# A gated feed forward in two phases: all up units first, then a down-projection with resident weights

## The chip, the cores and the metric

One core of one Trainium2 chip runs the whole step: one layer of a streaming encoder for 1,024 frames of a prompt and 128 frames of running streams, 1,152 columns in all. The metric is the device time of one execution in microseconds. TensorE multiplies, ScalarE and VectorE and GpSimd work element by element, SyncE issues the DMA transfers.

## The reference

Only the last part of the layer is touched by the change:

```python
h2 = rmsnorm(x, norm_ffn)                       # (T, 1024)
up = h2 @ w_up                                  # (T, 5632) = gate and value, 2816 each
c, conv_new = causal_dwconv(up, conv_left, conv_w, conv_b)   # width 3, per channel
gate, val = jnp.split(c, [D_FF], axis=-1)
x = x + (jax.nn.gelu(gate) * val) @ w_down      # w_down (2816, 1024)
y = rmsnorm(x, norm_final)
```

All is float32. The kernel splits every operand of a product into a high and a low part (types F32R) and adds three products, high by high, high by low and low by high: `mm3`, L117 to L121, three matmuls, one per line from L119 to L121. The split of a weight is a cast on ScalarE (L95) and a subtraction on GpSimd (L96), called "ap"; with "ad" the subtraction is on VectorE. An activation is split by L86 (ScalarE) and L87 (VectorE).

## The kernel before

The 2,816 hidden channels are 22 blocks of 128, m = 0 to 21. For each m, `up_unit` (L1292) loads two weight columns of 512 KB (gate and value), multiplies them with the normed input (`mh0`, `ml0`, `mh12`, `ml12`, resident in SBUF) in three chunks of 384 columns, 24 matmuls each, copies the result to E, applies the convolution on VectorE (L1313, L1314) into C, then gelu, product (L1320) and split into gh and gl, 128 hidden channels by 1,152 columns.

The down-projection takes two blocks m at a time (`down_group`, L1358). It loads their two rows of weights (512 KB each, all 1,024 outputs), and for each of the nine column tiles t and both halves of the outputs it makes a chain of six matmuls of 512 columns into one PSUM bank. VectorE adds the bank to `x1` (L1370), the residual, which stays in SBUF. The loop at the end of the kernel runs a group after every second up unit:

```python
for m in range(NU):
    up_unit(m)
    if m >= 2 and m % 2 == 0 and m < NU - 2:
        down_group([m - 2, m - 1])
    if m == NU - 1:
        down_group([NU - 4, NU - 3])
```

The group of m = 20 and 21 is the last work, and in it the final norm of each tile t follows its last addition (`final_norm` L1326, `final_half` L1335 for the last tile, whose norm is made in halves).

Raw weights pass through two buffers, the split ones through three (`load_w` L98, pool `wp`). PSUM gives `dn` four banks. All loads and stores are issued by SyncE in one order. A scheduler sets the order of the instructions on each engine; pools and buffer counts set when a tile may be overwritten.

Of the kernel before, what the change touches and what calls it, by code (L numbers as in the profile page):

```python
# [39 lines left out]
def trunk_kernel(  # L40
# [1285 lines left out]
    def final_norm(t):  # L1326
        yo = p6.tile([P, D], F32, tag="C", bufs=3, name=f"yo{t}")
        rs = rms_scale(p6, x1[t], yo, f"y{t}")

        def scale():  # L1330
            tc.keep_in_program_order(dve.scalar_tensor_tensor(yo, x1[t], rs, gfin, ALU.mult, ALU.mult))
            store_rows(yo, t, y_prompt[0], y_sample.rearrange("b t d -> t b d"))
        return scale

    def final_half(t, hf, part, pend):  # L1335
        hs = slice(hf * 512, (hf + 1) * 512)
        if hf == 0:
            part["yo"] = p6.tile([P, D], F32, tag="E", bufs=3, name=f"yo{t}")
            part["xg"] = p6.tile([P, D], F32, tag="E", bufs=3, name=f"xg{t}")
        yo, xg = part["yo"], part["xg"]  # L1340
        ssq = p6.tile([P, 1], F32, tag="ssq", bufs=4, name=f"ssq_y{t}_{hf}")
        act.activation(yo[:, hs], x1[t][:, hs], AF.Square, accum_out=ssq)
        (dve if hf else pool).tensor_tensor(xg[:, hs], x1[t][:, hs], gfin[:, hs], ALU.mult)
        if hf:
            pend()
        rs = p6.tile([P, 1], F32, tag="rs", bufs=4, name=f"rs_y{t}_{hf}")
        pool.tensor_scalar(rs, ssq, 1.0 / D, part["rs"] if hf else EPS, ALU.mult, ALU.add)
        if hf == 0:
            part["rs"] = rs
            return  # L1350
        pool.tensor_tensor(rs, rs, neg_half, ALU.pow)
        dve.tensor_scalar(yo[:, 0:512], xg[:, 0:512], rs, None, ALU.mult)
        act.activation(yo[:, hs], xg[:, hs], AF.Copy, scale=rs)
        for h_ in range(2):
            o = slice(h_ * 512, (h_ + 1) * 512)
            store_rows(yo[:, o], t, y_prompt[0, :, o], y_sample[:, :, o].rearrange("b t d -> t b d"))

    def down_group(ms, last=False):  # L1358
        ws = [load_w(lambda r: [(r, w_down[0, m * P:(m + 1) * P, :])], [D], f"wd{m}") for m in ms]
        part = {}  # L1360
        for t in range(NT):
            tk = slice(t * P, (t + 1) * P)
            for hf in range(2):
                ps = psp.tile([P, 512], F32, tag="tp" if hf else "pj", bufs=2, name=f"dn{ms[0]}_{t}_{hf}")
                hs = slice(hf * 512, (hf + 1) * 512)
                for i, m in enumerate(ms):
                    gh, gl = gts[m]
                    wh, wl = ws[i]
# [77 lines left out]
```

## Time and profile before

| | |
|---|---|
| median of 3 runs | 1756.23 us (1755.69 to 1756.74) |
| profiled execution | 1757.64 us |
| its span in the profile | 1755.9 us, so 1.7 us lie around it |
| TensorE busy | 1718.8 us, 98% |
| VectorE, ScalarE, GpSimd busy | 884.6, 744.3, 447.7 us |
| DMA | 125 MB, 71 GB/s over the span |

"Busy" counts the time in which an engine executes; matmuls overlap each other, so the distance from start to start of two matmuls tells their cost, not the length of one. In a row of the timeline, what stands in brackets is the time that the engine was idle before, and what it waited for.

### The profile page before, as it was taken

The page shows a single profiled execution, that of the slowest core. Times are in us where ns is not written, and L with a number is a line of the kernel's source. Part 1 is how long each engine was busy: PE and PEld are TensorE (multiplying, and loading weights), DVE is VectorE, ACT ScalarE, POOL GpSimd, SP SyncE. Part 2 cuts the span into 40 slices and gives each one's busy share as a digit, 9 for nine tenths or more (in the row PEclk, how much of TensorE's full clock was granted, in tenths as well). Part 3 has the DMA queues.
Part 4 walks back from the last instruction along what each step waited for, and adds up shares of the span by engine and source line. Part 5 has one row for each costly group of instructions (what it writes and reads, how often), then busy time and mean ns, then how long its engine had stood idle before and what let it go on. Part 6 is the DMA issues. An engine that isn't in the chain of part 4 may idle for free.

```text
span 1755.9 us, 24096 instructions
## 1 busy us (share of the span) xinstructions
PE 1718.8 (98%) x9721; PEld 1563.8 (89%) x9721; DVE 884.6 (50%) x1226; ACT 744.3 (42%) x1448; POOL 447.7 (25%) x508
## 2 busy tenths in 40 slices
PE   8999999999999999999999999999999999999997
PEld 7999998888798887888889898989989899898995
DVE  5350016778777775554244534445353443535356
ACT  5231117778776776543334232423323232232323
POOL 4111233211223103314313131312213131222222
PEclk9999999999999999999999999999999999999999
DMA  6112131111113127656301111111101111111112
GB/s 186 49 46 68 63 101 55 40 47 40 59 43 97 56 72 265 212 191 193 94 1 37 35 49 49 37 49 36 52 25 61 36 49 37 37 52 36 49 37 111
DMA packets 131660, 125.10 MB, mean 71 GB/s; under 512 B 7345, under 2 KB 111741, under 8 KB 131549
## 3 DMA queue, kind: packets, MB, share of 16 engines
q1 hardware_dynamic: 131549, 123.57, 22.1%
q8 instruction: 76, 1.25, 0.3%
q14 instruction: 35, 0.29, 0.1%
HBM read 101.63 MB, written 21.65 MB: 70 GB/s over the span
## 4 chain that ended last, share of the span: by engine, by line
PE 78%; DVE 12%; ACT 4%; DMA 2%; issue 2%; POOL 1%; SPq 0%; POOLq 0%; ACTq 0%; DVEq 0%
PE up L121 10%; PE up L120 10%; PE up L119 10%; PE dn L119 4%; PE dn L120 4%; PE dn L121 4%; DVE S L603 3%; PE gb L120 2%; PE gb L121 2%; PE gb L119 2%; PE avs L813 2%; PE zs L783 2%; PE ga L119 2%; PE ga L121 1%; PE o L119 1%
## 5 line engine op out<-in xcount | busy, mean ns | idle before, releaser
L119 PE MATMUL up<-mh,wup_h 128*128 128x384 f32 x1056 | 353.4, 335 | 0.0
L121 PE MATMUL up<-mh,wup_l 128*128 128x384 f32 x1056 | 353.0, 334 | 0.0
L120 PE MATMUL up<-ml,wup_h 128*128 128x384 f32 x1056 | 352.8, 334 | 0.0
L1313 DVE SCALAR_TENSOR_TENSOR C<-E,convp,C 128x128 f32<-128x128 f32 x88 | 81.0, 921 | 286.6 <-ACT C L1310 286.6
L1370 DVE TENSOR_TENSOR x<-dn,x 128x512 f32<-128x512 f32 x198 | 132.8, 687 | 149.8 <-PE dn L121 149.7
L119 PEld LDWEIGHTS up<-mh,wup_h 128*128 128x128 f32 x1056 | 198.4, 188 | 0.5
L120 PEld LDWEIGHTS up<-ml,wup_h 128*128 128x128 f32 x1056 | 198.3, 188 | 0.3
L121 PEld LDWEIGHTS up<-mh,wup_l 128*128 128x128 f32 x1056 | 198.2, 188 | 0.0
L96 POOL TENSOR_TENSOR wup_l<-wup_r,wup_h 128x1024 fp32r<-128x1024 f32 x44 | 105.1, 2398 | 283.6 <-ACT wup_h L95 244.2
L119 PE MATMUL dn<-wd_h,gh 128*128 128x512 f32 x396 | 158.3, 401 | 2.0 <-DVE x L1370 2.0
L120 PE MATMUL dn<-wd_l,gh 128*128 128x512 f32 x396 | 156.5, 395 | 1.4 <-POOL wd_l L96 1.4
L121 PE MATMUL dn<-wd_h,gl 128*128 128x512 f32 x396 | 156.3, 395 | 0.0
L95 ACT CAST wup_h<-wup_r 128x1024 fp32r<-128x1024 f32 x44 | 45.5, 1049 | 212.7 <-PE dn L121 143.2
L1309 ACT COPY E<-up 128x384 f32<-128x384 f32 (+2 forms) x176 | 65.7, 399 | 151.0 <-PE up L121 151.0
L1314 DVE SCALAR_TENSOR_TENSOR C<-E,convp,C 128x1024 f32<-128x1024 f32 x88 | 112.0, 1273 | 0.0
L119 PEld LDWEIGHTS dn<-wd_h,gh 128*128 128x128 f32 x396 | 74.2, 188 | 26.0 <-DVE x L1370 9.2
L120 PEld LDWEIGHTS dn<-wd_l,gh 128*128 128x128 f32 x396 | 74.3, 188 | 18.5 <-POOL wd_l L96 1.9
L121 PEld LDWEIGHTS dn<-wd_h,gl 128*128 128x128 f32 x396 | 74.3, 188 | 18.0
L1310 ACT ACTIVATE C<-up,convp 128x384 f32<-128x384 f32 x132 | 90.0, 681 | 0.0
L601 DVE SCALAR_TENSOR_TENSOR e<-z,e 128x384 f32<-128x384 f32 (+3 forms) x96 | 53.2, 555 | 66.2 <-ACT e L598 65.5
L119 PE MATMUL kv<-wkv_h,hTh 128*128 128x256 f32 x288 | 85.1, 296 | 0.6 <-DVE ql L502 0.5
L121 PE MATMUL kv<-wkv_h,hTl 128*128 128x256 f32 x288 | 81.4, 283 | 0.0
(296 smaller groups left out, 3889.8 us busy)
## 6 DMA issues: line engine op xcount, KB each, us to landing
wup_r<-in_w_up_dram SPq DMA_DIRECT2D x44, 512.0 KB
wd_r<-in_w_down_dram SPq DMA_DIRECT2D x22, 512.0 KB
v<-in_cache_v_dram SPq DMA_DIRECT2D x32, 256.0 KB
kr<-in_cache_k_dram SPq DMA_DIRECT2D x7, 1024.0 KB
sp_tb<-tb SPq DMA_DIRECT2D x8, 576.0 KB
out_dram<-kvst SPq DMA_DIRECT2D x72, 64.0 KB
sp_ga<-ga SPq DMA_DIRECT2D x24, 192.0 KB
tbr<-sp_tb SPq DMA_DIRECT2D x24, 192.0 KB
```

What stands on the lines that cost most here:

```text
L95: act.copy(hi, raw)
L96: (pool if how[1] == "p" else dve).tensor_tensor(lo, raw, f32(hi), ALU.subtract)
L119: pe.matmul(ps, lhsT=lh, rhs=rh, start=start, stop=False)
L120: pe.matmul(ps, lhsT=lh, rhs=rl, start=False, stop=False)
L121: pe.matmul(ps, lhsT=ll, rhs=rh, start=False, stop=stop)
L601: dve.scalar_tensor_tensor(ev, z, 0.0, ev, ALU.max, ALU.add)
L603: dve.tensor_tensor_scan(Sv[:, ::-1], ev[:, ::-1], ev[:, ::-1], init, ALU.add, ALU.bypass)
L1309: act.copy(d_, s2_)
L1310: act.activation(C[:, cs], ps, AF.Identity, scale=convp[:, 2, u:u + 1], bias=convp[:, 3, u:u + 1])
L1313: dve.scalar_tensor_tensor(C[:, 0:P], E[:, 16 - 8 * sh:EZ - 8 * sh], wv, C[:, 0:P], ALU.mult, ALU.add)
L1314: dve.scalar_tensor_tensor(C[:, P:T], E[:, EP - sh:EL - sh], wv, C[:, P:T], ALU.mult, ALU.add)
L1370: ins = dve.tensor_tensor(x1[t][:, hs], ps, x1[t][:, hs], ALU.add)
```

## The change

The feed forward becomes two phases.

- Up phase: all 22 up units in a row. Each product g (not split) is stored to `sp_g` in device memory, 22 stores of 576 KB. The residual `x1` is stored to `sp_x` when the norm ahead of the feed forward has read it (9 x 512 KB), and its room in SBUF is given up.
- Down phase: for half hf of the outputs and tile t one block, a chain of 66 matmuls (22 hidden blocks by 3) into one PSUM bank, in the order t = 0 to 8 for hf = 0, then again for hf = 1. Blocks (0,0) and (1,0) are interleaved in pieces. The weights of one half are resident in 11 pieces q of 512 KB (two hidden blocks each). For hf = 0 pieces 0 to 2 are loaded when m = 18 is done, 3 to 5 as the last up units give up the buffers of `wp`, 6 to 10 into a pool `pb` that lies where the input of the up phase was. For hf = 1 each piece is loaded again, split "ap", once block (8,0) has used the old one.
- For every block its g is loaded again from `sp_g`, in two chunks of 11 hidden blocks (128 rows of 11 runs of 512 bytes), and split (1,408 elements per partition, ScalarE and VectorE). Two sets of split tiles take turns, one in pool `pa`, one in `pb`.
- The residual comes back as `xr` (9 x 512 KB). In the second half every tile's norm is made in halves (`final_half`), the first half's sum of squares and product before the second half's addition.
- The order of TensorE's instructions in the down phase is that of the program (`manual_schedule`).

In the code of the change, `load_w` and `mm3` stand two lines lower (L100 and L119), the rest as the hunks say. What is left out at the first "..." is the old split into gh and gl, `final_norm`, the old `final_half` and `down_group`, all removed.

```diff
--- before.py
+++ after.py
@@ -72,6 +72,8 @@
 
     sp_tb = [dram.tile([P, T], F32, name=f"sp_tb{c}") for c in range(KD)]
     sp_ga = [dram.tile([P, T], F32, name=f"sp_ga{c}") for c in range(KD)]
+    sp_x = [dram.tile([P, D], F32, name=f"sp_x{t}") for t in range(NT)]
+    sp_g = dram.tile([P, NU, T], F32, name="sp_g")
     sp_at = [dram.tile([P, SEQ], F32, name=f"sp_at{c}") for c in range(4)]
 
     ident = cp.tile([P, P], F32, name="ident")
@@ -932,7 +934,8 @@
     s_h.close()
 
 
-    m12p = mk_pool("m12", "right")
+    s_m = ExitStack()
+    m12p = mk_pool("m12", "right", stack=s_m)
     C2 = T - CH
     mh12 = m12p.tile([P, KD, C2], F32R, name="mh12")
     ml12 = m12p.tile([P, KD, C2], F32R, name="ml12")
@@ -1157,10 +1160,11 @@
     s_at.close()
 
 
-    m0p = mk_pool("m0", "right")
+    m0p = mk_pool("m0", "right", stack=s_m)
     mh0 = m0p.tile([P, KD, CH], F32R, name="mh0")
     ml0 = m0p.tile([P, KD, CH], F32R, name="ml0")
-    xpool = mk_pool("x1", "right")
+    s_x = ExitStack()
+    xpool = mk_pool("x1", "right", stack=s_x)
     x1 = [xpool.tile([P, D], F32, name=f"x1_{t}") for t in range(NT)]
     s_wo = ExitStack()
     wop = mk_pool("wo", "right", stack=s_wo)
@@ -1274,6 +1278,7 @@
     conv_prep()
     for i, t in enumerate(TORD):
         out_mm(wo, 1, t)
+        sync.dma_start(sp_x[t], x1[t])
         norm2(t)
         if i >= 2:
             norm2_T(TORD[i - 2])
@@ -1281,14 +1286,17 @@
         norm2_T(t, False)
     s5.close()
     s_wo.close()
-
-
-    p6 = mk_pool("p6", "left")
+    s_x.close()
+
+
+    NP = NU // 2
+    PA, PW = 3, 3
+    pa = mk_pool("pa", "left")
+    s6 = ExitStack()
+    p6 = mk_pool("p6", "left", stack=s6)
     EZ = 16 + P
     EP = EZ + 2
     EL = EP + SEQ
-    gts = {}
-
     def up_unit(m):
         cc = []
         for s_ in range(2):
@@ -1317,63 +1325,32 @@
             pool.tensor_copy(convq[:, u, :], E[:, EL - 2:EL])
             cc.append(C)
         act.activation(cc[0], cc[0], AF.Gelu_apprx_tanh)
-        dve.tensor_tensor(cc[0], cc[0], cc[1], ALU.mult)
-        gh = p6.tile([P, T], F32R, tag="gh", bufs=3, name=f"gh{m}")
-        gl = p6.tile([P, T], F32R, tag="gl", bufs=3, name=f"gl{m}")
-        split(gh, gl, cc[0])
-        gts[m] = (gh, gl)
-
...
+        g = p6.tile([P, T], F32, tag="g", bufs=2, name=f"g{m}")
+        dve.tensor_tensor(g, cc[0], cc[1], ALU.mult)
+        sync.dma_start(sp_g[:, m, :], g)
+
+    wds = {}
+    pools = {}
+
+    def wd_load(q, hf):
+        alt = (pa, "dh", "dl", PA) if q < PA else (wp, "hi", "lo", 3) if q < PA + PW else \
+            (pools["b"], "dh", "dl", NP - PA - PW)
+        src = w_down[0, 2 * q * P:(2 * q + 2) * P, hf * 512:(hf + 1) * 512].rearrange("(j p) d -> p j d", p=P)
+        wds[q, hf] = load_w(lambda r: [(r, src)], [2, 512], f"wd{q}_{hf}", "ap" if q < PA or hf else "ad", alt)
+
+    gts = {}
+    GC = 11
+
+    def g_load(t, hf, m0, m1):
+        nm = f"g{t}_{hf}"
+        if (t, hf) not in gts:
+            gp = pools["b"] if (t + hf) % 2 else pa
+            gts[t, hf] = [gp.tile([P, NU, P], F32R, tag=f"gg{i}", bufs=1, name=f"{nm}_{i}") for i in range(2)]
+        gh, gl = gts[t, hf]
+        raw = pa.tile([P, GC, P], F32, tag="graw", bufs=2, name=f"{nm}_r{m0}")[:, :m1 - m0, :]
+        sync.dma_start(raw, sp_g[:, m0:m1, t * P:(t + 1) * P])
+        act.copy(gh[:, m0:m1, :], raw)
+        dve.tensor_tensor(gl[:, m0:m1, :], raw, f32(gh[:, m0:m1, :]), ALU.subtract)
 
     def conv_out(rows, n, stores, nm):
         ps = psp.tile([P, P], F32, tag="av", bufs=1, name=f"tr_{nm}")
@@ -1398,19 +1375,93 @@
 
     for m in range(NU):
         up_unit(m)
-        if m >= 2 and m % 2 == 0 and m < NU - 2:
-            down_group([m - 2, m - 1])
-        if m == NU - 1:
-            down_group([NU - 4, NU - 3])
         if m in (8, 16):
             conv_rows(0, m - 8)
             conv_rows(1, m - 8)
+        if m == 18:
+            for q in range(PA):
+                wd_load(q, 0)
+            g_load(0, 0, 0, GC)
+    s_m.close()
+
+
+    pb = mk_pool("pb", "right")
+    pools["b"] = pb
+    g_load(0, 0, GC, NU - 2)
+    g_load(1, 0, 0, GC)
+    for q in range(PA, NP - 1):
+        wd_load(q, 0)
+    g_load(1, 0, GC, NU - 2)
+    wd_load(NP - 1, 0)
+    g_load(0, 0, NU - 2, NU)
+    g_load(1, 0, NU - 2, NU)
     conv_rows(0, 16)
     conv_rows(1, 16)
     conv_last()
-    gfin = p6.tile([P, D], F32, tag="E", bufs=3, name="gfin")
+    s6.close()
+    p8 = mk_pool("p8", "left")
+    gfin = p8.tile([P, D], F32, name="gfin")
     sync.dma_start(gfin, norm_final.rearrange("(o d) -> o d", o=1).to_broadcast([P, D]))
-    down_group([NU - 2, NU - 1], last=True)
+    xr = [p8.tile([P, D], F32, name=f"xr{t}") for t in range(NT)]
+    for t in range(NT):
+        sync.dma_start(xr[t], sp_x[t])
+    dps = {}
+
+    def down_mm(t, hf, qs):
+        if qs[0] == 0:
+            dps[t, hf] = psp.tile([P, 512], F32, tag="tp" if t % 2 else "pj", bufs=2, name=f"dn{t}_{hf}")
+        gh, gl = gts[t, hf]
+        for q in qs:
+            wh, wl = wds[q, hf]
+            for j in range(2):
+                m = 2 * q + j
+                mm3(dps[t, hf], gh[:, m, :], gl[:, m, :], wh[:, j, :], wl[:, j, :], m == 0, m == NU - 1)
+
+    def down_add(t, hf):
+        hs = slice(hf * 512, (hf + 1) * 512)
+        dve.tensor_tensor(xr[t][:, hs], dps.pop((t, hf)), xr[t][:, hs], ALU.add)
+
+    fin = {}
+
+    def final_half(t, hf):
+        hs = slice(hf * 512, (hf + 1) * 512)
+        if hf == 0:
+            fin[t] = [p8.tile([P, D], F32, tag=tg, bufs=2, name=f"{tg}{t}") for tg in ("yo", "xg")]
+        yo, xg = fin[t][:2]
+        ssq = p8.tile([P, 1], F32, tag="ssq", bufs=4, name=f"ssq_y{t}_{hf}")
+        act.activation(yo[:, hs], xr[t][:, hs], AF.Square, accum_out=ssq)
+        (dve if hf else pool).tensor_tensor(xg[:, hs], xr[t][:, hs], gfin[:, hs], ALU.mult)
+        rs = p8.tile([P, 1], F32, tag="rs", bufs=4, name=f"rs_y{t}_{hf}")
+        pool.tensor_scalar(rs, ssq, 1.0 / D, fin[t][2] if hf else EPS, ALU.mult, ALU.add)
+        if hf == 0:
+            fin[t].append(rs)
+            return
+        pool.tensor_tensor(rs, rs, neg_half, ALU.pow)
+        dve.tensor_scalar(yo[:, 0:512], xg[:, 0:512], rs, None, ALU.mult)
+        act.activation(yo[:, hs], xg[:, hs], AF.Copy, scale=rs)
+        for h_ in range(2):
+            o = slice(h_ * 512, (h_ + 1) * 512)
+            store_rows(yo[:, o], t, y_prompt[0, :, o], y_sample[:, :, o].rearrange("b t d -> t b d"))
+
+    with tc.manual_schedule(engines={mybir.EngineType.PE}):
+        for qs in ((0, 1, 2), (3, 4), (5, 6), (7, 8), (9,), (10,)):
+            for t in (0, 1):
+                down_mm(t, 0, qs)
+        down_add(0, 0)
+        down_add(1, 0)
+        for hf in range(2):
+            for t in range(2 * (1 - hf), NT):
+                g_load(t, hf, 0, GC)
+                g_load(t, hf, GC, NU)
+                for q in range(NP):
+                    down_mm(t, hf, (q,))
+                    if hf == 0 and t == NT - 1:
+                        wd_load(q, 1)
+                if hf:
+                    final_half(t, 0)
+                down_add(t, hf)
+                if hf:
+                    final_half(t, 1)
 
 
 _INS = ['x_prompt', 'x_sample', 'cache_k', 'cache_v', 'state_pool', 'state_conv',
```

Three places of the order are spoken of below. The first is VectorE after the last up matmul. Before, it has the additions of `dn` around the last conv chain (E and C are the tiles of one up column):

```order
L1370 TENSOR_TENSOR x_0_8139<-dn_0_0_15011,x_0_8139 128x512
L1313 SCALAR_TENSOR_TENSOR C_14902<-E_14901,convp,C_14902 128x128
L1314 SCALAR_TENSOR_TENSOR C_14902<-E_14901,convp,C_14902 128x1024
L1313 SCALAR_TENSOR_TENSOR C_14902<-E_14901,convp,C_14902 128x128
L1314 SCALAR_TENSOR_TENSOR C_14902<-E_14901,convp,C_14902 128x1024
L1370 TENSOR_TENSOR x_0_8139<-dn_0_1_15019,x_0_8139 128x512
L1320 TENSOR_TENSOR C_14804<-C_14804,C_14902 128x1152
L1370 TENSOR_TENSOR x_1_8140<-dn_1_0_15027,x_1_8140 128x512
L1370 TENSOR_TENSOR x_1_8140<-dn_1_1_15035,x_1_8140 128x512
```

Now the same place has weight splits of pieces q (`wd_0`, half 0), the last conv chain, and the low parts of g for the first two blocks (`g_0_1`: half 0, low part):

```order
L98 TENSOR_TENSOR wd_0_l<-wd_0_r,wd_0_h 128x1024
L1321 SCALAR_TENSOR_TENSOR C_13503<-E_13502,convp,C_13503 128x128
L1322 SCALAR_TENSOR_TENSOR C_13503<-E_13502,convp,C_13503 128x1024
L1321 SCALAR_TENSOR_TENSOR C_13503<-E_13502,convp,C_13503 128x128
L1322 SCALAR_TENSOR_TENSOR C_13503<-E_13502,convp,C_13503 128x1024
L1353 TENSOR_TENSOR g_0_1_13608<-g_0_r_13609,g_0_0_13607 128x1408
L1329 TENSOR_TENSOR g_13595<-C_13405,C_13503 128x1152
L98 TENSOR_TENSOR wd_0_l<-wd_0_r,wd_0_h 128x1024 x2
L1353 TENSOR_TENSOR g_0_1_13608<-g_0_r_13655,g_0_0_13607 128x1152
```

The additions are gone from here; the low part of g for block (1,0) (first row with 128x1408) comes after the chain of the last up unit.

The second is ScalarE from the end of the first half on. `g_1_0` is the high part of g of half 1, `wd_1_h` that of a weight piece; nothing of this was there before:

```order
L1352 CAST g_0_0_14318<-g_0_r_14324 128x1408
L1352 CAST g_1_0_14462<-g_1_r_14464 128x1408
L1352 CAST g_1_0_14462<-g_1_r_14468 128x1408
L97 CAST wd_1_h<-wd_1_r 128x1024 x5
L1352 CAST g_1_0_14557<-g_1_r_14559 128x1408
L97 CAST wd_1_h<-wd_1_r 128x1024
L1352 CAST g_1_0_14557<-g_1_r_14563 128x1408
L97 CAST wd_1_h<-wd_1_r 128x1024 x5
L1352 CAST g_1_0_14652<-g_1_r_14654 128x1408
```

The casts of g for (0,1) come ahead of the weight casts, and those for (1,1) among them.

The third is GpSimd at the same place. Before, its last splits were spread between up units:

```order
L1317 COPY convq<-E_14803 128x2
L96 TENSOR_TENSOR wd_l<-wd_r,wd_h 128x1024
L1315 COPY convs<-E_14803 128x2x8
L1317 COPY convq<-E_14901 128x2
L96 TENSOR_TENSOR wd_l<-wd_r,wd_h 128x1024
L1315 COPY convs<-E_14901 128x2x8
L96 TENSOR_TENSOR wd_l<-wd_r,wd_h 128x1024
```

Now all eleven follow each other, and the norm of tile 0 (`rs_y_1`) is behind them:

```order
L1433 TENSOR_TENSOR xg_14540<-xr_13694,gfin 128x512
L1435 TENSOR_SCALAR rs_y_0_14544<-ssq_y_0_14541 128x1
L1433 TENSOR_TENSOR xg_14635<-xr_13695,gfin 128x512
L98 TENSOR_TENSOR wd_1_l<-wd_1_r,wd_1_h 128x1024 x11
L1435 TENSOR_SCALAR rs_y_1_14550<-ssq_y_1_14547,rs_y_0_14544 128x1
L1439 TENSOR_TENSOR rs_y_1_14550<-rs_y_1_14550,neg_half 128x1
```

The splits of half 1 stand in one row here, counted x11.

## Rows read from the trace of the kernel before

**Rows 1.** The page, head and part 1: busy us (share of span) x instructions.
```profile
span 1755.9 us, 24096 instructions
...
PE 1718.8 (98%) x9721; PEld 1563.8 (89%) x9721; DVE 884.6 (50%) x1226; ACT 744.3 (42%) x1448; POOL 447.7 (25%) x508
```

**Rows 2.** Table by stretches: start:end, us, busy us per engine (x instructions), PEclk, DMA share, GB/s.
```profile
1000.00:1100.00 100.00, 99.79 (x521) 92.03 (x520) 39.92 (x47) 27.53 (x45) 23.71 (x25) 1.00 0.14 43
...
1600.00:1700.00 100.00, 99.79 (x539) 94.53 (x537) 44.05 (x49) 33.80 (x56) 24.90 (x26) 1.00 0.13 43
```

**Rows 3.** The page, part 5: costliest groups, with count, busy us, mean ns, idle before.
```profile
L119 PE MATMUL up<-mh,wup_h 128*128 128x384 f32 x1056 | 353.4, 335 | 0.0
...
L119 PE MATMUL dn<-wd_h,gh 128*128 128x512 f32 x396 | 158.3, 401 | 2.0 <-DVE x L1370 2.0
```

**Rows 4.** Timeline of TensorE, first group of `dn`: start us, us, operation [idle before].
```profile
985.76 0.39 PE L119 MATMUL dn<-wd_h,gh 128*128 128x512 f32 x1
...
994.63 0.50 PE L119 MATMUL dn<-wd_h,gh 128*128 128x512 f32 x1 [0.20 <-DVE x L1370]
...
1011.54 0.34 PE L119 MATMUL up<-mh,wup_h 128*128 128x384 f32 x1
```

**Rows 5.** Timeline of TensorE, the last two groups of `dn`.
```profile
1693.10 0.39 PE L119 MATMUL dn<-wd_h,gh 128*128 128x512 f32 x1
...
1723.30 0.50 PE L120 MATMUL dn<-wd_l,gh 128*128 128x512 f32 x1 [1.44 <-POOL wd_l L96]
...
1746.04 0.39 PE L121 MATMUL dn<-wd_h,gl 128*128 128x512 f32 x1
```

**Rows 6.** Timeline of TensorE: a run of `dn` matmuls, and one of `o`.
```profile
885.10 0.39 PE L121 MATMUL o<-wo_h,ml 128*128 128x512 f32 x1
...
887.82 0.39 PE L121 MATMUL o<-wo_h,ml 128*128 128x512 f32 x1
...
1704.87 0.40 PE L119 MATMUL dn<-wd_h,gh 128*128 128x512 f32 x1
...
1706.27 0.40 PE L119 MATMUL dn<-wd_h,gh 128*128 128x512 f32 x1
```

**Rows 7.** Timelines of ScalarE, VectorE and GpSimd after the last up matmul.
```profile
1693.12 1.05 ACT L95 CAST wd_h<-wd_r 128x1024 fp32r<-128x1024 f32 x1 [2.93 <-PE up L120]
...
1694.49 0.69 ACT L1310 ACTIVATE C<-up,convp 128x384 f32<-128x384 f32 x1
...
1695.30 1.49 DVE L1313 SCALAR_TENSOR_TENSOR C<-E,convp,C 128x128 f32<-128x128 f32 x1
...
1697.91 0.34 DVE L1313 SCALAR_TENSOR_TENSOR C<-E,convp,C 128x128 f32<-128x128 f32 x1
1698.17 1.27 DVE L1314 SCALAR_TENSOR_TENSOR C<-E,convp,C 128x1024 f32<-128x1024 f32 x1
...
1699.97 1.34 DVE L1320 TENSOR_TENSOR C<-C,C 128x1152 f32<-128x1152 f32 x1
...
1694.24 2.40 POOL L96 TENSOR_TENSOR wd_l<-wd_r,wd_h 128x1024 fp32r<-128x1024 f32 x1 [4.39 <-ACT wd_h L95]
```

**Rows 8.** SyncE's queue, one weight load; its traffic by stretches; a full burst.
```profile
1040.13 0.38 SPq L104 DMA_DIRECT2D wup_r<-in_w_up_dram  x1
...
1043.00:1043.50 0.50, 0.50 (x5) 0.50 (x4) 0.50 (x1) 0.00 (x0) 0.44 (x2) 1.00 0.24 69
...
670.00:675.00 5.00, 3.77 (x19) 3.03 (x20) 3.91 (x9) 4.11 (x11) 0.00 (x0) 1.00 1.04 396
```

**Rows 9.** Timelines of GpSimd and VectorE in the last two groups and at the end.
```profile
1720.49 2.76 POOL L96 TENSOR_TENSOR wd_l<-wd_r,wd_h 128x1024 fp32r<-128x1024 f32 x1 [23.64 <-ACT wd_h L95]
...
1746.47 0.69 DVE L1370 TENSOR_TENSOR x<-dn,x 128x512 f32<-128x512 f32 x1 [0.31 <-PE dn L121]
...
1746.48 1.27 POOL L1343 TENSOR_TENSOR xg<-x,gfin 128x512 f32<-128x512 f32 x1
...
1749.70 0.55 POOL L1351 TENSOR_TENSOR rs_y<-rs_y,neg_half 128x1 f32<-128x1 f32 x1
```

More of the change, by code (lines that the diff above doesn't have):

```diff
@@ L1319, in up_unit @@
         act.activation(cc[0], cc[0], AF.Gelu_apprx_tanh)
-        dve.tensor_tensor(cc[0], cc[0], cc[1], ALU.mult)
-        gh = p6.tile([P, T], F32R, tag="gh", bufs=3, name=f"gh{m}")
-        gl = p6.tile([P, T], F32R, tag="gl", bufs=3, name=f"gl{m}")
-        split(gh, gl, cc[0])
-        gts[m] = (gh, gl)
[L1326 to L1368, printed above, removed]
-                    mm3(ps, gh[:, tk], gl[:, tk], wh[:, hs], wl[:, hs], i == 0, i == len(ms) - 1)
-                ins = dve.tensor_tensor(x1[t][:, hs], ps, x1[t][:, hs], ALU.add)
-                if last and t == NT - 1:
-                    final_half(t, hf, part, pend)
-            if last and t < NT - 1:
-                if t:
-                    pend()
-                pend = final_norm(t)
+        g = p6.tile([P, T], F32, tag="g", bufs=2, name=f"g{m}")
```

## The prediction

> **What bounds the kernel now.** I read the page's head first. TensorE is busy for 1718.8 of 1755.9 us, and the other engines for half of that or less [rows 1]. The table by stretches says the same of the feed forward: 99.8% in the first full stretch of 100 us and in the last, 1000 to 1100 and 1600 to 1700, at the full granted clock (2.4 GHz), with DMA at 0.13 to 0.14 [rows 2]. So the stage ends when TensorE has done its matmuls, and a change can win only by making them closer, by taking away their small waits, or by shortening what follows the last of them. It loses by every wait it adds. The groups give the count: 3168 matmuls of `up`, 1188 of `dn` [rows 3]. The profiled execution took 1757.64 us, 1.4 above the median of 1756.23; I work in differences and add them to the median.
>
> **What the down-projection costs now.** A group takes 25.78 us, from 985.76 to the next up matmul at 1011.54 [rows 4]; nine stand alone, and the last two take 53.2 us, from 1693.10 to 0.23 after 1746.04 [rows 5]. Together 9 x 25.78 + 53.2 = 285.2 us. At the spacing of undisturbed ones, 6 in 1.40 us or 0.2333 each [rows 6], 1188 would take 277.2. The other 8.0 us are waits: for L1370's additions, which free the PSUM banks but stand behind the conv chain on VectorE (994.63), and once 1.44 us for a split on GpSimd (1723.30) [rows 4, 5].
>
> **The change, part by part.** The count of matmuls is the same.
>
> *Spacing.* A chain grows from 6 to 66 matmuls. The same 512-column shape runs in the `o` projection with 12 steps in 2.72 us, 0.2267 each [rows 6]. Nothing in the trace says what makes the difference. Both operands of `dn` come to lie elsewhere, so part of it may go. Bounds 0.2267 (269.3 us) and 0.2333 (277.2); I take the middle, 0.230: 273.2 us. The waits for PSUM go too, as one bank serves 15.2 us (66 x 0.230) and its addition takes 0.69 [rows 9].
>
> *Up phase.* The units keep their matmuls. New there are 22 stores of g, 9 of x1, three weight splits and one g load. DMA has 86% of its time free [rows 2], and each store waits for an operation that other work needs anyway; the splits cost GpSimd 3 x 2.40 us in stretches where it is busy for a quarter. If this cover failed, a unit would wait for its weights, which still have two raw buffers. I count nothing.
>
> *A, the end of the up phase.* Let L be the end of the last up matmul. TensorE then has 18 matmuls of block (0,0), 4.1 us, and with some transposes and two matmuls of (1,0) that use the high part alone 4.9 us, before it needs the low part of g of (1,0). Its tiles lie where the up phase's input lay and are free only at L. The order shows its subtraction on VectorE behind the last conv chain. ScalarE's cast (1.05), copies and affine take until 2.1 us after L [rows 7]; the chain then needs 0.34 + 1.27 + 0.34 + 1.27 = 3.2, or 1.2 more if its first operation takes 1.49 as it did before. The subtraction is my estimate from the 1.34 us at 1152 elements: 1.34 x 1408 / 1152 = 1.64. That is L + 7.0 to 8.4, less 4.9 of cover: 2.1 to 3.5; with hops 1.5 to 3.8, **2.5 us** taken.
>
> *B, block (2,0).* Its g takes the tiles of (0,0), which ends only 6 matmuls (1.4 us) before (1,0). After that come a cast (1.05 x 1408 / 1024 = 1.44, an estimate) and the subtraction, behind two additions and a square: about 5 us, of which 1.8 are covered. This gives at least 3.0. The raw g is also behind nine loads of 512 KB of x1 on SyncE; at the 390 GB/s of a full burst [rows 8] these take 12.1 us, and they can start only some 18 to 21 us after L, while the two blocks end at about L + 33. I take **4.7 us** of 3.0 to 6.5. All later blocks have 15.2 us in which to turn g (6.2 us of ScalarE and VectorE), so they wait for nothing.
>
> *C, the change of halves.* Block (0,1) needs the second half of the weights, and each piece may be overwritten only when block (8,0), 15.2 us long, has used it. All 11 go through two raw buffers and GpSimd. Such a load is issued at 1040.13; its traffic ends by about 1043.3, so 3.2 us [rows 8]. Cast 1.05, split 2.40 [rows 7], 0.2 of hops: a buffer comes round in 6.85 us. With S the start of (8,0), ScalarE first casts g of (0,1) (2 x 1.44), then piece 0 at S + 2.9, whose low part is ready at S + 6.35. Piece 10 is five turns later, S + 40.6; TensorE wants it at S + 15.2 + 60 x 0.230 = S + 29.0. That is 11.6 us, and 1.4 more for the cast of g (1,1), which the order puts among the weight casts: **13.0 us**. From below: if transfers cost nothing, GpSimd alone needs 11 x 2.40 after S + 3.95, S + 30.4, 1.4 us late. From above: 3.5 us a transfer, the slower split of 2.76 [rows 9], both g casts: S + 44.2 + 2.8, 18.0 us late. The first is far off since it takes the load out; I keep near the measured one.
>
> *A rule to weigh here.* The split on GpSimd from 1694.24 to 1696.64 lies over the 1.49 us operation on VectorE, and the same operation took 0.34 once GpSimd was done [rows 7]. The Trainium skill, SBUF — State Buffer, section "SBUF: two separate sides", says that a VectorE operation with two SBUF inputs and a GpSimd operation exclude each other through a lock; the trace agrees (1.49 against 0.34). The sum has no term for such turns, since VectorE has only four g subtractions while the 11 splits run; rival 3 gives their price.
>
> *Tail.* Now the end waits for the second half's statistics on GpSimd, which stand behind a 1.27 us product there: last addition 1746.47, scale ready 1750.25 [rows 9]. The change computes the first half of the norm a half-phase earlier, so this product is gone: **1.2 us** gained (0.5 to 1.5). Store and end are as before.
>
> **Sum.** 273.2 + 2.5 + 4.7 + 13.0 = 293.4 against 285.2 is +8.2; less 1.2 is +7.0, so 1756.2 + 7.0 = **1763 us**. With the lower ends (269.3, 1.5, 3.0, 11.6, tail 1.5) it is 1755, with the upper ones (277.2, 3.8, 6.5, 18.0, 0.5) 1776.
>
> **Rivals.**
> 1. *Faster: the weights arrive.* Loads and splits overlap so well at the change of halves that GpSimd's 26.4 us alone decide, and C is 1.4. This holds if a buffer comes round in 4.8 us or less, that is a load in 1.2 us. With 269.3 to 273.2, A 2.5 and B 3.0 to 4.7 it gives 1745 to 1751, say 1748. For it: DMA is all but idle there. Against it: the 3.2 us of a load in a quiet stretch [rows 8].
> 2. *No change.* The matmuls take the `o` spacing throughout: 269.3 + 2.5 + 4.7 + 11.6 = 288.1, +2.9 - 1.2: 1758. For it: `o` [rows 6]. Against: the old `dn` never reached it, though its two last groups ran on without up units.
> 3. *Slower still: GpSimd and VectorE take turns.* Each of the four subtractions lengthens the chain of splits by its 1.64 us: C 19.6, 1770. It decides if VectorE's subtractions fall into the splits rather than into GpSimd's pauses (2.05 of each 6.85 us). Going by the rule of the page named above, this is the time.
>
> **How the numbers follow.** The forecast has 0.55, the rivals 0.15, 0.17 and 0.13. A measurement of this kernel can tell about 0.2%, 3.5 us, from no change. Faster, below 1752.7, is rival 1: 0.15. Within are rival 2 and the forecast's low end (0.08): 0.25. Slower 0.60. The range 1750 to 1776 leaves out most of rival 1 and what lies above all upper ends, under 0.2 together; the forecast's own is 1755 to 1776.
>
> **What would show it.** Per step: the distance of `dn` matmuls within a chain (0.227 to 0.233); a wait of 2 to 4 us of TensorE on VectorE's g subtraction some 5 us after the last up matmul; one of 3 to 6 at the start of (2,0); in (0,1), waits at every second piece on the GpSimd split (L98), summing to 12 to 18 us, with splits 2.4 us long and about 3.4 apart. The prediction is wrong if block (0,1) runs through with less than 5 us of waits, if a wait stands in the up phase, or if the clock of the stage is not 1.00.

## Result and the profile after

The changed kernel takes 1767.34 us (median of 4 runs, 1765.93 to 1769.51) against 1756.03 us for the kernel before beside it: ratio 1.0063, 95% interval 1.0049 to 1.0077. It is slower by 11.3 us, where 7.0 had been forecast. The span of its profiled execution is 1767.7 us, 11.8 more than before.

The head of the page and the groups of `dn` answer to [rows 1, 3]; after the bar stands the idle time ahead of a group and what ended it:

```profile
span 1767.7 us, 24261 instructions
...
PE 1721.3 (97%) x9721; PEld 1568.7 (89%) x9721; DVE 808.3 (46%) x1078; ACT 774.3 (44%) x1488; POOL 454.4 (26%) x516
...
L122 PE MATMUL dn<-wd_l,g 128*128 128x512 f32 x396 | 159.4, 402 | 8.7 <-POOL wd_l L98 8.6
L121 PE MATMUL dn<-wd_h,g 128*128 128x512 f32 x396 | 158.8, 401 | 3.6 <-ACT g L1352 2.8
L123 PE MATMUL dn<-wd_h,g 128*128 128x512 f32 x396 | 158.6, 401 | 1.8 <-DVE g L1353 1.8
```

The matmuls are as many as before, and the waits have other releasers: low parts of weights on GpSimd, g on ScalarE and VectorE. The additions (L1422) are gone from the list. The table by stretches answers to [rows 2] and shows where it happens (busy us of PE, PEld, DVE, ACT, POOL, then PEclk, DMA share, GB/s):

```profile
1000.00:1100.00 100.00, 100.00 (x578) 100.00 (x578) 38.75 (x36) 38.18 (x69) 28.58 (x41) 1.00 0.20 67
...
1400.00:1500.00 100.00, 94.77 (x490) 87.08 (x488) 42.59 (x43) 37.77 (x62) 17.30 (x23) 0.98 0.48 166
1500.00:1600.00 100.00, 99.90 (x422) 81.25 (x423) 28.03 (x22) 20.87 (x17) 2.78 (x1) 0.97 0.37 108
1600.00:1700.00 100.00, 90.53 (x370) 70.74 (x369) 26.82 (x23) 30.44 (x40) 38.92 (x27) 0.95 0.48 149
```

The up phase is full, at the full clock. The losses are in 1400 to 1500 (the first two blocks) and in 1600 to 1700 (the change of halves), and the granted clock is below 1.00 in all three stretches of the down phase, even in 1500 to 1600, where TensorE is busy for 99.9%. That was not forecast. The starts of blocks, from TensorE's timeline, give each term its size:

```profile
1460.93 0.48 PE L121 MATMUL dn<-wd_h,g 128*128 128x512 f32 x1
...
1495.28 0.39 PE L123 MATMUL dn<-wd_h,g 128*128 128x512 f32 x1
...
1498.44 0.50 PE L121 MATMUL dn<-wd_h,g 128*128 128x512 f32 x1 [2.77 <-ACT g L1352]
1498.77 0.54 PE L122 MATMUL dn<-wd_l,g 128*128 128x512 f32 x1
1500.10 0.79 PE L123 MATMUL dn<-wd_h,g 128*128 128x512 f32 x1 [0.78 <-DVE g L1353]
1500.69 0.63 PE L121 MATMUL dn<-wd_h,g 128*128 128x512 f32 x1
1501.12 0.63 PE L122 MATMUL dn<-wd_l,g 128*128 128x512 f32 x1
...
1517.64 0.39 PE L121 MATMUL dn<-wd_h,g 128*128 128x512 f32 x1
...
1532.75 0.39 PE L121 MATMUL dn<-wd_h,g 128*128 128x512 f32 x1
...
1548.06 0.39 PE L121 MATMUL dn<-wd_h,g 128*128 128x512 f32 x1
...
1608.90 0.39 PE L121 MATMUL dn<-wd_h,g 128*128 128x512 f32 x1
...
1639.13 0.39 PE L121 MATMUL dn<-wd_h,g 128*128 128x512 f32 x1
...
1760.55 0.39 PE L123 MATMUL dn<-wd_h,g 128*128 128x512 f32 x1
```

The stage runs from 1460.93 to 0.23 after 1760.55, 299.85 us against 285.2, so 14.65 more. Undisturbed blocks take 15.11 and 15.31 us in turn (1517.64 to 1532.75 to 1548.06). With nine of each, 273.8 us:

| term | forecast | measured | from |
|---|---|---|---|
| 1188 matmuls | 273.2 | 273.8 | 9 x 15.11 + 9 x 15.31 |
| A, first two blocks | 2.5 | 4.2 | 1460.93 to 1495.51 is 34.58, less 132 x 0.2305 |
| B, block (2,0) | 4.7 | 6.8 | 1495.51 to 1517.64 is 22.13, less 15.31 |
| C, block (0,1) | 13.0 | 15.1 | 1608.90 to 1639.13 is 30.23, less 15.11 |
| tail | -1.2 | -2.7 | last matmul to end 7.15, was 9.86 |

In block (2,0) one sees more than its two waits: after them the matmuls come 0.427 us apart, about twice the 0.23, until 1505.8. The granted clock there is 0.50, its lower level (1.2 GHz):

```profile
1500.00:1502.00 2.00, 1.90 (x5) 1.52 (x6) 1.64 (x2) 0.37 (x1) 0.00 (x0) 0.50 0.34 101
1502.00:1504.00 2.00, 2.00 (x6) 1.61 (x5) 0.03 (x1) 0.00 (x0) 0.00 (x0) 0.50 1.12 336
...
1636.00:1638.00 2.00, 2.00 (x5) 1.15 (x4) 0.00 (x0) 0.00 (x0) 1.03 (x1) 0.50 0.00 0
```

In all, 27 of the distances in this execution are 0.42 to 0.43 us: 6 after the waits of A, 11 here, and 10 in block (0,1), where the clock is at 0.50 for longest, from 1628.6 to 1638.8. In the trace of before it is 1.00 through the whole stage.

C was forecast from the turn of a raw buffer. The timelines of ScalarE, GpSimd and VectorE in it:

```profile
1604.09 1.05 ACT L97 CAST wd_h<-wd_r 128x1024 fp32r<-128x1024 f32 x1 [5.99 <-DMA wd_r<-in_w_down_dram]
1607.19 1.05 ACT L97 CAST wd_h<-wd_r 128x1024 fp32r<-128x1024 f32 x1 [2.05 <-DMA wd_r<-in_w_down_dram]
...
1612.51 2.40 POOL L98 TENSOR_TENSOR wd_l<-wd_r,wd_h 128x1024 fp32r<-128x1024 f32 x1 [1.80 <-ACT wd_h L97]
1615.51 3.09 POOL L98 TENSOR_TENSOR wd_l<-wd_r,wd_h 128x1024 fp32r<-128x1024 f32 x1 [0.60 <-ACT wd_h L97]
...
1613.73 2.65 DVE L1353 TENSOR_TENSOR g<-g_r,g 128x1408 fp32r<-128x1408 f32 x1 [3.94 <-ACT g L1352]
1616.73 3.35 DVE L1353 TENSOR_TENSOR g<-g_r,g 128x1408 fp32r<-128x1408 f32 x1 [0.34 <-ACT g L1352]
```

ScalarE waits for the load before each cast from piece 2 on, and two subtractions of g, 1.62 us long elsewhere, take 2.65 and 3.35 beside the splits, one of which takes 3.09 instead of 2.40. They take turns rather than slow each other down: the subtraction begun at 1616.73 ends at 1620.08, 1.48 us after the split that ends at 1618.60. The last split ends at 1637.0, 43.4 us after block (8,0) began; 42.0 had been forecast (40.6, and 1.4 for the cast of g (1,1)). Its load shows how long a raw buffer waits for its data: issue, the end of its traffic, cast.

```profile
1629.85 0.37 SPq L106 DMA_DIRECT2D wd_r<-in_w_down_dram  x1
...
1633.00:1633.50 0.50, 0.00 (x0) 0.00 (x0) 0.00 (x0) 0.00 (x0) 0.50 (x1) 0.50 0.02 4
...
1633.55 1.04 ACT L97 CAST wd_h<-wd_r 128x1024 fp32r<-128x1024 f32 x1 [1.82 <-DMA wd_r<-in_w_down_dram]
```

The traffic is over by 1633.0, about 3.2 us after the issue as forecast, but the cast begins 3.70 us after it. No load of g had been issued since 1622.77.

### The profile page after: what moved, and what is told of

The parts are those of the page before. It is cut to its first block, busy times and chain, and to the rows that moved or that the text cites. A ratio compares the mean times of both kernels' runs of the same rounds, so it can differ in the third digit from the quotient of the medians.

```text
span 1767.7 us, 24261 instructions
## 1 busy us (share of the span) xinstructions
PE 1721.3 (97%) x9721; PEld 1568.7 (89%) x9721; DVE 808.3 (46%) x1078; ACT 774.3 (44%) x1488; POOL 454.4 (26%) x516
## 3 DMA queue, kind: packets, MB, share of 16 engines
q8 instruction: 76, 1.25, 0.3%
## 4 chain that ended last, share of the span: by engine, by line
PE 40%; issue 6%; DMA 2%; POOL 1%; ACT 1%; DVE 1%; SPq 0%; POOLq 0%; DVEq 0%; ACTq 0%
PE up L123 10%; PE up L122 10%; PE up L121 10%; PE dn L122 2%; PE dn L123 2%; PE dn L121 2%; DMA wd_r<-in_w_down_dram 2%; POOL wd_l L98 1%; PE o L123 1%; PE o L122 1%; PE o L121 1%; DMA xr<-sp_x 0%; ACT wd_h L97 0%; PE tr_f L150 0%; SPq L1351 0%
## 5 line engine op out<-in xcount | busy, mean ns | idle before, releaser
L1321 DVE SCALAR_TENSOR_TENSOR C<-E,convp,C 128x128 f32<-128x128 f32 x88 | 77.0, 875 | 312.1 <-ACT C L1318 303.8
L122 PE MATMUL dn<-wd_l,g 128*128 128x512 f32 x396 | 159.4, 402 | 8.7 <-POOL wd_l L98 8.6
L121 PE MATMUL dn<-wd_h,g 128*128 128x512 f32 x396 | 158.8, 401 | 3.6 <-ACT g L1352 2.8
L123 PE MATMUL dn<-wd_h,g 128*128 128x512 f32 x396 | 158.6, 401 | 1.8 <-DVE g L1353 1.8
L1352 ACT CAST g<-g_r 128x1408 fp32r<-128x1408 f32 (+2 forms) x38 | 49.0, 1306 | 139.3 <-PE dn L122 132.4
L122 PEld LDWEIGHTS dn<-wd_l,g 128*128 128x128 f32 x396 | 76.1, 192 | 29.1 <-POOL wd_l L98 12.1
L121 PEld LDWEIGHTS dn<-wd_h,g 128*128 128x128 f32 x396 | 76.2, 192 | 21.9 <-ACT g L1352 3.2
L123 PEld LDWEIGHTS dn<-wd_h,g 128*128 128x128 f32 x396 | 76.2, 192 | 19.7 <-DVE g L1353 2.5
L1422 DVE TENSOR_TENSOR xr<-dn,xr 128x512 f32<-128x512 f32 x18 | 12.4, 692 | 169.8 <-PE dn L123 169.8
```

The costliest lines, as they stand in the source:

```text
L121: pe.matmul(ps, lhsT=lh, rhs=rh, start=start, stop=False)
L122: pe.matmul(ps, lhsT=lh, rhs=rl, start=False, stop=False)
L123: pe.matmul(ps, lhsT=ll, rhs=rh, start=False, stop=stop)
L1321: dve.scalar_tensor_tensor(C[:, 0:P], E[:, 16 - 8 * sh:EZ - 8 * sh], wv, C[:, 0:P], ALU.mult, ALU.add)
L1352: act.copy(gh[:, m0:m1, :], raw)
L1422: dve.tensor_tensor(xr[t][:, hs], dps.pop((t, hf)), xr[t][:, hs], ALU.add)
```

## Experiments

Nine kernels ran, one of them twice, each beside the kernel before, which took 1755.6, 1757.4 and 1756.8 us in the three sets. Times of different sets are compared by their ratios.

**1. Without the reload** (`no_reload`; the second half is computed with the first half's weights, so that half of the result is another).

```diff
-                        wd_load(q, 1)
+                        wds[q, 1] = wds[q, 0]
```

> The second half of the outputs is multiplied with the weights of the first half, so 11 loads of 512 KB and 11 splits on GpSimd are left out, and with them everything that block (0,1) waited for. Theory (the reload is what block (0,1) waits for, 15.0 us of its 30.2): block (0,1) takes 15.1 to 15.4 us, and the time falls from 1767.3 to 1752 to 1753. Rival (another wait of the change of halves takes its place, such as g of (0,1) or the norms that start there): block (0,1) still takes over 20 us, and the time stays above 1757.

Measured: 1752.56 us, ratio 0.9982 (0.9971 to 0.9994). Block (0,1) takes 15.11 us, from 1606.89 to the start of (1,1):

```profile
1606.89 0.39 PE L121 MATMUL dn<-wd_h,g 128*128 128x512 f32 x1
...
1622.00 0.39 PE L121 MATMUL dn<-wd_h,g 128*128 128x512 f32 x1
```

So C is the reload's, all 15 us of it, and no other wait takes its place. Without C the change would be a small gain, with A and B still in it.

**2. The splits on VectorE** (`split_on_vector`): in `wd_load` "ad" instead of "ap" for the second half.

```diff
-        wds[q, hf] = load_w(lambda r: [(r, src)], [2, 512], f"wd{q}_{hf}", "ap" if q < PA or hf else "ad", alt)
+        wds[q, hf] = load_w(lambda r: [(r, src)], [2, 512], f"wd{q}_{hf}", "ap" if q < PA and not hf else "ad", alt)
```

> Second half's low parts of the weights on VectorE instead of GpSimd, nothing else. Theory (a raw buffer comes round in load 3.2 + cast 1.05 + split, so a split of 1.2 instead of 2.4 shortens the turn from about 6.9 to 5.7 us): piece 10 is ready some 7 us sooner, block (0,1) waits about 8 us instead of 15, time about 1760. Rival (the transfers decide, in a memory system that is fuller than I took it to be): block (0,1) still waits over 12 us, time 1764 or more. Rival (GpSimd's lock with VectorE is the whole loss): block (0,1) waits under 3 us, time 1755.

Measured: 1771.47 us, ratio 1.0078 (1.0059 to 1.0098), no gain; the profiled execution (1766.40) was the fastest of its four, and what made the others 4 to 6 us longer is not shown. In it block (0,1) takes 28.08 us. SyncE's queue shows why the shorter split bought little, and the table by stretches the traffic behind it:

```profile
1610.95 1.90 SPq L1351 DMA_DIRECT2D g_r<-sp_g  x2
1613.62 15.49 SPq L106 DMA_DIRECT2D wd_r<-in_w_down_dram  x5
```

```profile
1616.00:1620.00 4.00, 0.59 (x3) 0.16 (x1) 0.00 (x0) 0.00 (x0) 0.00 (x0) 1.00 1.07 357
```

```profile
1620.38 1.04 ACT L97 CAST wd_h<-wd_r 128x1024 fp32r<-128x1024 f32 x1 [6.53 <-DMA wd_r<-in_w_down_dram]
```

The scheduler put both loads of g for (2,1), 1.44 MB that were not cast before 1635.97, ahead of piece 6, whose cast began only at 1620.38, 6.8 us after its issue. DMA is full meanwhile, and hardly any engine works. The turn of 5.7 us that was expected failed at the load, taken as 3.2: the second expectation holds.

**3. A third raw buffer** (`three_raw`; pieces 2, 5 and 8 of the second half take a raw tile of their own in pool p8, splits stay on GpSimd).

```diff
+        raw = (rawp or wp).tile([P] + shape, F32, tag="raw", bufs=1 if rawp else 2, name=f"{name}_r")
...
+                            pools.get("c") if hf and q % 3 == 2 else None)
```

> The changed kernel with a third raw buffer for the second half's weights; the splits stay on GpSimd. Theory (two buffers with turns of 7.3 us set C): three buffers allow one piece in 2.4 us, now set by GpSimd's split; piece 10 is ready near S + 33 instead of S + 43.4, block (0,1) waits 4 to 7 us instead of 15, time 1757 to 1760. Rival (the loads of g that stand between the weights on SyncE's queue, and their traffic, decide): block (0,1) still waits over 10 us, 1763 or more.

Measured: 1759.88 us, ratio 1.0015 (1.0005 to 1.0025). Block (0,1) takes 21.56 us, so it loses 6.4 instead of 15.1. Two buffers were what set C, as the forecast had it. What is left is GpSimd's, by the waits of TensorE in this stretch (who waited for whom: us in total, times, longest):

```profile
PE dn L122 <- POOL wd_l L98: 5.0, 5, 2.0
```

**4. Residual loads later** (`x1_late`): two of the nine stay, seven are issued after g of (2,0).

```diff
-    for t in range(NT):
+    for t in range(2):
         sync.dma_start(xr[t], sp_x[t])
...
+                if hf == 0 and t == 2:
+                    for t_ in range(2, NT):
+                        sync.dma_start(xr[t_], sp_x[t_])
```

> Of the nine loads of the residual only the first two stay ahead of the loads of g of block (2,0), seven come behind them. Theory (of the 2.9 and 1.1 us that TensorE waits at the start of (2,0), about 1.2 and 0.6 are the g loads behind the residual's; the rest is cast and subtraction after the tile comes free): the two waits shrink to 1.5 to 2.5 together, and the stretch at half clock after them (2.7 us) gets shorter or goes; time 1763 to 1765.5. Rival (the wait is all the tile's own, since the cast stands behind the addition and the square): no change, 1767.

Measured: 1764.26 us, ratio 1.0042 (1.0028 to 1.0057), in the expected band; its interval overlaps the changed kernel's, so the trace has to decide. The start of (2,0) no longer waits (1493.62 follows the last matmul of (1,0)), one wait for the low part of g is left, and the slow stretch is shorter: eight slow distances, not thirteen.

```profile
1496.08 0.50 PE L123 MATMUL dn<-wd_h,g 128*128 128x512 f32 x1 [1.73 <-DVE g L1353]
```

So part of B was the queue, as forecast.

**5. The wait filled with work** (`filled_wait`): TensorE gets 24 matmuls of 384 columns, result thrown away, between blocks (1,0) and (2,0).

```diff
+        dum = psp.tile([P, CH], F32, tag="z", bufs=3, name="dum")
+        for i in range(24):
+            pe.matmul(dum, lhsT=wds[NP - 1, 0][0][:, 0, 0:P], rhs=gts[1, 0][0][:, 0:3, :], start=i == 0, stop=i == 24 - 1)
```

> The changed kernel with 24 extra matmuls of 384 columns (about 4.2 us, result thrown away) on TensorE between block (1,0) and block (2,0), where it otherwise waits 2.9 + 1.1 us. Theory (the clock falls to 1.2 GHz because TensorE idled): no matmul of (2,0) comes 0.427 us apart, the 13 slow ones of the changed kernel cost 2.7 us, so 1764 to 1765 although work is added. Rival (the slow stretch has another cause, such as the full DMA traffic at that moment): matmuls of (2,0) are still 0.427 apart, 1767 to 1768.

Measured: 1765.62 us, ratio 1.0045 (1.0031 to 1.0059); the intervals of this ratio and of the changed kernel's overlap, so the time alone does not decide. The trace does. TensorE's timeline:

```profile
1493.40 4.35 PE L1452 MATMUL dum<-g,wd_h 128*128 128x384 f32 x24
1497.67 0.50 PE L121 MATMUL dn<-wd_h,g 128*128 128x512 f32 x1
...
1499.33 0.50 PE L123 MATMUL dn<-wd_h,g 128*128 128x512 f32 x1 [0.93 <-DVE g L1353]
1499.67 0.39 PE L121 MATMUL dn<-wd_h,g 128*128 128x512 f32 x1
1499.90 0.40 PE L122 MATMUL dn<-wd_l,g 128*128 128x512 f32 x1
```

The table by stretches (the last three columns are PEclk, DMA share and GB/s):

```profile
1500.00:1502.00 2.00, 2.00 (x11) 1.63 (x10) 1.26 (x1) 0.00 (x0) 0.00 (x0) 1.00 0.71 203
1502.00:1504.00 2.00, 2.00 (x10) 1.65 (x9) 0.00 (x0) 0.25 (x1) 0.00 (x0) 1.00 1.07 310
```

The g of (2,0) comes no sooner, DMA is as full as in the changed kernel (there 0.34 and 1.12, here 0.71 and 1.07), and yet the clock stays at 1.00 and the matmuls 0.23 apart. So the slow stretch in B comes from TensorE's idleness, not from the traffic. Block (0,1), whose waits were not filled, still has its slow stretches (the clock is at 0.50 from 1616.6 to 1626.8 and from 1630.2 to 1633.6).

**6. Equal addresses, old order** (`before_aligned`, and once more as `before_aligned_again`).

```diff
+        if m == 0:
+            p6.tile([P, 48], F32, name="gpad")
         gh = p6.tile([P, T], F32R, tag="gh", bufs=3, name=f"gh{m}")
```

> The kernel before with one change: a gap of 192 bytes ahead of gh and gl in SBUF, so that both operands of the down-projection start at the same address modulo 256. In the changed kernel the 593 matmuls with equal addresses modulo 256 came 0.227 us apart and the 594 with unequal ones 0.234. Theory (the equality sets the distance): all 1188 at 0.227 in the old order with its short chains too, 1188 x 0.0066 = 7.9 us less, 1748. Rival (the length of the chain or another circumstance of the new order sets it): 0.233 as before, 1756.

Measured: 1751.31 us, ratio 0.9967 (0.9950 to 0.9984). A run of the same 6-matmul chains now reads:

```profile
1699.91 0.39 PE L119 MATMUL dn<-wd_h,gh 128*128 128x512 f32 x1
...
1701.27 0.39 PE L119 MATMUL dn<-wd_h,gh 128*128 128x512 f32 x1
```

Six in 1.36 us, 0.227 each, where [rows 6] had 1.40. The chain's length has nothing to do with it. Of the 7.9 us calculated the `dn` stretches keep 4.9: the waits longer than 0.26 us grow from 7.9 to 9.7, probably because VectorE's additions come no sooner (argued, not tried).

**7. Equal addresses, new order** (`after_aligned`): a gap of 224 bytes at the head of pool `pa`.

```diff
     pa = mk_pool("pa", "left")
+    pa.tile([P, 56], F32, name="apad")
```

> The changed kernel with a gap of 224 bytes at the head of pool pa, so that all operands of the down-projection have the same address modulo 256. Theory: the 594 matmuls that came 0.234 apart come 0.227 apart, 594 x 0.007 = 4.0 us less, except where a wait takes it back (block (0,1) waits for weights anyway, 0.2), about 1763.5. Rival (only the old order reacts so): no change, 1767.

Measured: 1766.63 us, ratio 1.0055 (1.0042 to 1.0068), 3 us above the expectation and no gain that the intervals can tell. The undisturbed blocks all take 14.96 us, so the spacing follows the addresses here too. But block (0,1) takes 32.80 us and the wait ahead of (2,0) is 1.3 us longer: the gain went into waits for weights and g that are timed by other engines. The weights came 2 us later still, counted from the start of (8,0): the loads of pieces 4 and 8 took 4.7 and 5.1 us from issue to cast, where the changed kernel had 3.8 and 4.0. Why was not tried. The clock is at its lower level for longer, too, and into block (1,1), which takes 15.81:

```profile
1620.00:1636.00 16.00, 12.14 (x26) 8.16 (x27) 0.78 (x2) 4.38 (x4) 8.80 (x4) 0.50 0.39 118
```

**8. All repairs** (`all_repairs`): 4 and 7 together, a third raw buffer with the splits taken in turn by GpSimd and VectorE, and the first two blocks in other pieces.

```diff
-        wds[q, hf] = load_w(lambda r: [(r, src)], [2, 512], f"wd{q}_{hf}", "ap" if q < PA or hf else "ad", alt)
+        wds[q, hf] = load_w(lambda r: [(r, src)], [2, 512], f"wd{q}_{hf}", ("ad" if q % 2 else "ap") if hf else "ap" if q < PA else "ad", alt,
+                            pools.get("c") if hf and q % 3 == 2 else None)
...
-        for qs in ((0, 1, 2), (3, 4), (5, 6), (7, 8), (9,), (10,)):
+        for qs in ((0, 1, 2, 3), (4,), (5, 6), (7, 8, 9, 10)):
...
+                if qs[-1] == 10:
+                    down_add(t, 0)
```

> The changed kernel with every repair: equal addresses modulo 256, seven residual loads behind g of (2,0), block (0,0) finished four pieces ahead of (1,0), four pieces before the first wait, a third raw buffer with splits taken in turn by GpSimd and VectorE. Theory: 1188 x 0.227 = 269.7 us, A 1 to 2, B 0 to 1, C 0 to 3, tail 2.7 less than before: 285.2 falls to 271 to 276, time 1741 to 1745, faster than both kernels and than the old order with equal addresses (1751). Rival (two phases cost a wait at each seam whatever is repaired): 1750 or more.

Measured: 1743.54 us, ratio 0.9932 (0.9912 to 0.9951), as expected for the time, and faster than both kernels. By stretches: first two blocks, the rest of the first half, block (0,1), the rest:

```profile
1457.00:1488.00 31.00, 30.43 (x134) 24.43 (x133) 17.64 (x18) 14.08 (x20) 3.48 (x3) 1.00 0.74 234
1488.00:1593.00 105.00, 105.00 (x465) 86.97 (x464) 32.78 (x24) 24.26 (x20) 8.78 (x4) 1.00 0.55 162
1593.00:1612.00 19.00, 15.61 (x68) 12.30 (x67) 9.07 (x6) 8.17 (x8) 9.85 (x4) 1.00 0.76 230
1612.00:1732.00 120.00, 119.98 (x530) 99.02 (x528) 37.17 (x38) 34.27 (x54) 25.27 (x31) 1.00 0.36 108
```

B is gone, A is 1.5 us (31.46 from 1457.00 to the start of (2,0), less 2 x 14.96), C 4.0 (18.93 less 14.96; 0 to 3 had been expected), and the clock is 1.00 in all four stretches.

**9. All repairs, splits on VectorE alone** (`repairs_vector`), with the old order beside it. The edit is against `all_repairs`:

```diff
-        wds[q, hf] = load_w(lambda r: [(r, src)], [2, 512], f"wd{q}_{hf}", ("ad" if q % 2 else "ap") if hf else "ap" if q < PA else "ad", alt,
+        wds[q, hf] = load_w(lambda r: [(r, src)], [2, 512], f"wd{q}_{hf}", "ap" if q < PA and not hf else "ad", alt,
```

> All repairs, but the second half's low parts all on VectorE, none on GpSimd. In the trace of all repairs three of six GpSimd splits took 3.2 to 3.7 us and three of five VectorE splits 2.0 to 3.3 us, where these lay over each other. Theory (the two engines shut each other out): without GpSimd every split takes 1.2 us and every subtraction of g 1.6, none over 1.7. The loads of pieces 9 and 10 now stand behind both loads of g of (2,1) on SyncE's queue, so block (0,1) may still wait 1 to 4 us for those two; time 1741 to 1745, no loss against all repairs. Rival (VectorE gets its long durations from the DMA traffic): splits still spread to 2 us and more.

> The old order with equal addresses, beside the repaired two-phase kernel on one chip. Theory: the two phases then gain what the old order loses in waits for the additions, about 8 us, and 2.7 at the end: 1750 here against 1741 to 1745. Rival (equal addresses are the whole gain): both within 3 us.

Measured: 1744.54 us, ratio 0.9930 (0.9908 to 0.9953), against 1751.95, ratio 0.9971 (0.9958 to 0.9983). The two phases, once repaired, are 7.4 us ahead of the old order with equal addresses, so the rival of the second expectation (within 3 us) falls. Groups of splits in `all_repairs` (first two lines) and in `repairs_vector` (third), over the same stretch:

```profile
L98 POOL TENSOR_TENSOR wd_l<-wd_r,wd_h 128x1024 fp32r<-128x1024 f32 x6 | 17.3, 2898 | 102.3 <-ACT wd_h L97 102.3
...
L98 DVE TENSOR_TENSOR wd_l<-wd_r,wd_h 128x1024 fp32r<-128x1024 f32 x5 | 10.0, 1992 | 10.8 <-ACT wd_h L97 10.7
```

```profile
L98 DVE TENSOR_TENSOR wd_l<-wd_r,wd_h 128x1024 fp32r<-128x1024 f32 x11 | 13.3, 1223 | 12.5 <-ACT wd_h L97 12.2
```

Mean 1992 and 2898 ns where both engines split, 1223 where one does; the rival (traffic) falls. Block (0,1) loses 7.5 us here, more than the 1 to 4 expected: 4.7 are waits at piece 9, which stood behind g of (2,1), and the rest is the stretch at the lower clock that follows them (0.50 from 1610.9 to 1617.7). The ratio shows no loss by it against `all_repairs` within its interval.

## Why the prediction was right, point by point

- **Range and number.** 1767.3 lies in the range, but 4 us above the 1763 forecast and only 3 below the 1770 of rival 3; the terms, not the sum, have to say which mechanism it was.
- **One sign of being wrong did show.** The prediction called itself wrong if the clock of the stage was not 1.00. It was 0.50 in three stretches (1468.1 to 1471.6, 1498.9 to 1505.7, 1628.6 to 1638.8). The sum has no term for that, and this is the one mechanism that it lacks: it stands in A, B and C below.
- **Sign and place: right.** A, B and C are where the loss is, and nothing stands in the up phase: `dn` begins 0.15 us earlier than nine old groups of 25.78 less would give (1460.93 against 1693.10 - 232.02).
- **Spacing: right in size, open in cause.** 273.8 for 273.2. I took the middle of two spacings since the trace did not say which holds. Both hold, half and half: the 594 matmuls whose two operands start at equal addresses modulo 256 are 0.227 apart, the other 594 0.234. Experiments 6 and 7 show the cause. The `o` matmuls of [rows 6] fit it, with both operands at 224.
- **C: right in mechanism, 2.1 short.** Two raw buffers set it (experiments 1, 3). The term that was short is the load in "a buffer comes round in 6.85 us". Splits 0 and 10 ended 36.7 us apart, 7.33 per turn, because the cast began 3.6 to 4.0 us after the issue of each of the five loads between them; the 3.2 had been read at the end of the traffic. That made the last split 2.8 us later. GpSimd and VectorE taking turns added about 0.9 (split 0 took 3.15 us and split 6 2.60), so rival 3, which priced this at 6.6, had a small part of it. Against that, the 1.4 for the cast of g (1,1) was not paid, since both casts fell into ScalarE's waits for loads; that was luck, and smaller terms gave back another 0.9. So the last split came 1.4 late. The other 0.7 is the clock: the five matmuls behind that split took 2.04 us, where five after a wait at the full clock take 1.25. The waits in the block add up to 9.4 us, not to the 12 to 18 that were to show it; part of the rest passed in slow matmuls. The Trainium skill, SBUF — State Buffer, section "SBUF: two separate sides", states that VectorE operations with two SBUF inputs and GpSimd operations that read SBUF exclude each other; experiment 9 agrees with it: 1223 ns alone, 1992 side by side.
- **B: right in mechanism, 2.1 short.** The waits of 2.8 and 0.8 us were of the forecast kind. The step that failed is the one left out, that a matmul after a wait costs what it did before it. Thirteen distances at the lower clock (the eleven and one at each edge) cost 2.7 us (5.66 us instead of 13 x 0.23), and experiment 5 shows that idleness brings it on.
- **A: 1.7 short**, for the same reason: after its two waits of 0.8 and 1.0 us the nine distances from 1467.81 to 1471.74 took 3.93 us, not 2.07. The clock fell after A in this execution and in those of `split_on_vector` and `after_aligned`, and not in those of `no_reload`, `x1_late`, `filled_wait` and `three_raw`. What decides that was not found. It changes the total less than A alone: in `no_reload`, where the clock held, A cost 2.6 us, but the wait ahead of (2,0) was 4.19 us instead of 2.77, and A and B together cost 10.3 us instead of 11.0.
- **Tail: 1.5 better.** From the last matmul to the scale on GpSimd it is 2.94 us, was 4.21: the 1.2 as forecast. The rest is after it; before, tile 7's rows came out of VectorE at 1749.5 and their store stood just ahead of the last ones. That share is argued, not tried.
- **Rivals.** Rival 1 (weights arrive in time) needed a turn of 4.8 us and had 7.33; by its own terms it gives 1746 to 1752, not 1745 to 1751. (A's upper end has a slip of the same size: 2.1, 4.4 and 1.64 make L + 8.1, not 8.4. Neither moves the forecast.) Rival 2 (the `o` spacing throughout, 1758) was right about what spacing is possible, and `after_aligned` shows that alone it returns little here: ratio 1.0055 against 1.0063, which the intervals do not tell from nothing.

## What to carry to other kernels

Before a change that keeps TensorE in long chains, count for each seam the buffers that must come round, with the load counted until the cast can begin and as it will be behind everything else on its queue; a third buffer was worth 8 us here, a faster split by itself none. TensorE's waits at one seam cost 2.7 us more in matmuls at the lower clock, so price a wait with what follows it. Look at the distance of matmuls of one shape in several stages: where it differs, compare the operands' addresses, since a gap of 192 bytes was worth 5 us.
